# Staging the compressed-key tokens in a ring of four tiles, and nine new durations in the emission estimate of a four-mixer decoder layer

## The chip, the core and the metric

The kernel runs on one core of a Trainium2 chip. The metric is the device time of one execution, in microseconds. The engines are named as the profile names them: PE is TensorE (PEld its weight loads), DVE is VectorE, ACT is ScalarE, POOL is GpSimd, and SP is SyncE, whose queue issues all DMAs here.

## What is computed

One layer over 2048 tokens of width 1024: a normalised input times one combined projection, four groups of four heads, a gate, and an output projection added to the input.

```python
h = rms_norm(x, norm_w) @ w_in          # columns split among the four groups and the gate
o_a = dilated_attention(...)            # A: windows 128/1, 512/4, 2048/16, merged by their softmax sums
o_b = banded_attention(..., 127, sink)  # B: sliding window with sinks
o_c = diff_attention(...)               # C: two causal softmax maps, p0 - lam * p1
# D: three branches of one head group, weighted with sigmoid gates
kc, vc = compress(d_kc, ...), compress(d_vc, ...)        # 127 compressed keys and values
o_cmp = softmax(q @ kc.T + bias) @ vc
idx = top_k(sum over heads of the compressed weights, 16) # 16 of 32 blocks of 64 keys
o_slc = softmax over the selected blocks;  o_win = banded_attention(..., 511)
y = concat(o_a, o_b, o_c, o_d) * silu(gate)
x = x + y @ w_out
```

`compress` adds a position term to the raw keys and values of group D in two versions (one for the first 16 tokens of a block of 32, one for the last 16) and puts them through a small network.

## The kernel before

All engines' instructions are emitted by one program that keeps an estimate of each engine's clock (`T["PE"]`, `T["DVE"]` and so on). `op(engine, ns, after)` advances an estimate, and returns when a result would be there. The time given to `op` costs the chip nothing; it decides only **in which order** the instructions are written into the engines' queues. `defer(ready, f)` puts work off until TensorE's estimate passes `ready`. `drive` runs the attention units of a group and chooses, at each step, among the candidates that the estimate holds for ready: closing a unit, the products with the values, the transposes of the weights, the next scores. Only when none is ready by the estimate does `fill_step` put in a piece of a filler. Fillers are the projection of the groups (`project`: three matmuls for each of eight 128-row pieces of the width, line 833, written C, D, A, B) and the output projection (line 2148). Since every engine works its queue in order, a wrong estimate becomes a wait on the chip.

The stages follow each other so: the projection of C alone, then group C with the projections of C, D and the start of A as fillers, group D (window branch, compressed branch at line 1428, selected branch at line 943 with `Qs`), and groups A and B, with the output projection as filler.

Tiles that are written again and again are rings. `alloc(tag, bufs)` and `release` keep the estimate's record of when a ring's oldest tile comes free. Three rings matter here:

- `sq`, one tile of 128x512. Each projected row tile is squared into it by ACT (line 664) and summed by DVE (line 674).
- `raw`, four tiles of 128x512. The weights of the projections are loaded into them before they are split in a high and a low part (lines 618 and 622), and later the output weights and the gate.
- `pt`, three PSUM banks, for all transposes.

For every fourth row tile of the projection, `turn` transposes four row tiles into a `pt` bank. For the last column block of group D (raw keys and values) the inner function `version(v, e)` adds the position term into an `sq` tile (line 775, DVE), stores it to DRAM (`tc`, through SP), and only when that store has landed by the estimate does the second version take `sq`; then the `pt` bank is given back. This happens four times: blocks p = 0 to 3.

In the compressed branch, `largest` (lines 1471 to 1483, on DVE) chooses the blocks of keys of 128 queries, and `turn_ng` transposes the result (line 1489). `weigh` works out the branch's weights (lines 1277 and 1278), and `o_turn` turns the output back (line 435) and adds its two halves, either on DVE alone (line 439) or on ACT and DVE (lines 442 and 444), whichever the estimate holds to be done first.

## Time and profile before

| | |
|---|---|
| median of three runs | 1796.22 us (1788.68 to 1797.0) |
| the profiled execution, its own time | 1786.75 us |
| span from its first to its last instruction | 1785.0 us |
| busy: PE, DVE, ACT, POOL | 1715.9, 1332.7, 1072.1, 688.4 us |
| mean granted clock of TensorE | 0.986 of full speed |

The profile is of one execution. Between its first and its last instruction lie 1785.0 us, and 1.75 us of its time lie outside. An engine's busy time is the time in which it has an instruction running; what is left of the span is time in which it waits.

### The profile page before, as it was taken

What the parts mean: (1) busy time and instruction counts of PE and PEld (TensorE: products, weight loads), DVE (VectorE), ACT (ScalarE), POOL (GpSimd) and SP (SyncE); (2) the same over time, 40 slices, a digit from 0 to 9 for tenths busy, and PEclk for the clock granted to TensorE, in tenths of its full rate; (3) what the DMA queues carried; (4) which work ended last, traced back from release to release, by engine and by line L of the source; (5) the groups of instructions that cost most, each with busy time, mean ns of one, the idle gap of its engine ahead of it and who ended that gap; (6) DMA issues with size and microseconds to landing.
All of it is one profiled execution on the core that took longest, in us unless ns stands there. A gap on an engine that the chain in (4) does not pass through costs nothing.

```text
span 1785.0 us, 31766 instructions
## 1 busy us (share of the span) xinstructions
PE 1715.9 (96%) x10035; PEld 1503.3 (84%) x10035; DVE 1332.7 (75%) x4072; ACT 1072.1 (60%) x2586; POOL 688.4 (39%) x841
## 2 busy tenths in 40 slices
PE   7989999999998999899989999999999999999999
PEld 5878878888787888688877889999879998888887
DVE  5446778998899996688567778887167777888883
ACT  4445556666676765567555667676256776576661
POOL 4666564544454554112353632222521111423231
PEclk9999999999999999999998999999999999999999
DMA  7763554344446324831485333323375768999986
GB/s 244 227 206 115 165 170 159 99 125 138 125 130 202 100 93 144 229 102 57 142 250 180 123 93 86 109 62 96 103 239 163 233 209 266 293 326 304 303 280 215
DMA packets 283480, 308.24 MB, mean 173 GB/s; under 512 B 80256, under 2 KB 201216, under 8 KB 282640
## 3 DMA queue, kind: packets, MB, share of 16 engines
q1 hardware_dynamic: 283312, 306.21, 55.7%
q8 instruction: 80, 1.31, 0.3%
q14 instruction: 88, 0.72, 0.1%
HBM read 219.47 MB, written 86.92 MB: 172 GB/s over the span
## 4 chain that ended last, share of the span: by engine, by line
PE 44%; DMA 4%; DVE 4%; issue 3%; POOL 2%; SPq 1%; ACT 1%; POOLq 0%; DVEq 0%; ACTq 0%
PE o L422 8%; PE j L833 8%; PE j L2148 7%; PE pt L393 7%; PE s L943 4%; PE s L1639 3%; PE pt L435 2%; PE s L1329 1%; DMA wb<-tkA 1%; SPq L156 1%; DMA DQ<-tqD 1%; PE s L1428 1%; PE pt L2112 1%; POOL xl L577 1%; PE s L1941 0%
## 5 line engine op out<-in xcount | busy, mean ns | idle before, releaser
L833 PE MATMUL j<-wb,xh 128*128 128x512 f32 (+2 forms) x2048 | 619.4, 383 | 12.6 <-ACT wb L618 8.0
L833 PEld LDWEIGHTS j<-wb,xh 128*128 128x128 f32 x2048 | 372.4, 191 | 58.6 <-issue 12.2
L833 PE MATMUL j<-wb,xl 128*128 128x512 f32 (+2 forms) x1024 | 386.1, 377 | 1.3 <-POOL xl L577 1.3
L403 DVE TENSOR_TENSOR pl<-pt,ph 128x512 fp32r<-128x512 f32 (+4 forms) x486 | 312.0, 659 | 40.6 <-ACT ph L399 40.2
L399 ACT ACTIVATE ph<-pt 128x512 fp32r<-128x512 f32 (+4 forms) x486 | 265.3, 575 | 123.5 <-PE pt L393 116.8
L833 PEld LDWEIGHTS j<-wb,xl 128*128 128x128 f32 x1024 | 194.7, 190 | 27.7 <-POOL xl L577 2.7
L679 POOL TENSOR_TENSOR ss<-ss,expo 128x6 f32<-128x6 f32 (+2 forms) x64 | 117.1, 1829 | 213.6 <-DVE ss L677 202.3
L577 POOL TENSOR_TENSOR xl<-xt,xh 128x512 fp32r<-128x512 f32 x112 | 150.1, 1340 | 9.3
L371 ACT ACTIVATE ot<-o 128x512 f32<-128x512 f32 (+1 forms) x160 | 81.5, 509 | 108.9 <-PE o L422 108.4
L943 PE MATMUL s<-keys,Q 128*128 128x512 f32 (+3 forms) x320 | 113.1, 400 | 10.9 <-DVE mx L945 5.5
L2102 POOL TENSOR_TENSOR xt<-xt,sq 128x512 f32<-128x512 f32 x32 | 41.3, 1289 | 197.9 <-DVE sq L2100 85.8
L571 POOL TENSOR_SCALAR xh<-xt 128x512 fp32r<-128x512 f32 x128 | 85.5, 668 | 76.4 <-DMA xt<-in_xt_dram 47.5
L660 ACT ACTIVATE stqk<-j 128x512 f32<-128x512 f32 x64 | 38.3, 598 | 122.5 <-PE j L833 122.3
L945 DVE CUSTOM_DVE_ANT_0 prow<-s,Hs 128x512 f32<-128x512 f32 (+3 forms) x160 | 94.6, 606 | 18.1 <-PE s L943 11.4
L674 DVE TENSOR_REDUCE ss<-sq 128x6 f32<-128x384 f32 (+2 forms) x64 | 39.4, 616 | 92.0 <-ACT sq L664 91.9
L1059 DVE SCALAR_TENSOR_TENSOR pa<-pb,ra,pa 128x1024 f32<-128x1024 f32 (+4 forms) x96 | 103.5, 1105 | 2.3
L945 DVE CUSTOM_DVE_ANT_0 pa<-s,H 128x512 f32<-128x512 f32 (+3 forms) x160 | 93.7, 604 | 14.4 <-PE s L943 12.6
L1655 ACT ACTIVATE ap<-ap,AO 128x128 f32<-128x128 f32 (+1 forms) x192 | 86.4, 454 | 18.6 <-DVE AO L1649 16.7
L945 DVE CUSTOM_DVE_ANT_0 pb<-s,H 128x512 f32<-128x512 f32 (+3 forms) x160 | 92.8, 604 | 4.3 <-PE s L943 3.5
L435 PE MATMUL pt<-ident,ot 128*128 128x128 f32 x512 | 85.4, 279 | 5.2 <-ACT ot L371 5.0
L1043 ACT ACTIVATE pa<-pa,nm 128x128 f32<-128x128 f32 (+7 forms) x64 | 76.9, 1201 | 21.6 <-DVE nm L951 21.1
L1523 ACT ACTIVATE prow<-prow,nm 128x128 f32<-128x128 f32 (+7 forms) x64 | 76.8, 1201 | 15.3 <-DVE nm L951 7.3
(266 smaller groups left out, 4201.7 us busy)
## 6 DMA issues: line engine op xcount, KB each, us to landing
xt<-in_xt_dram SPq DMA_DIRECT2D x128, 256.0 KB, 3.5
xr<-in_x_dram SPq DMA_DIRECT2D x16, 512.0 KB, 5.6
Q<-tqC SPq DMA_DIRECT2D x64, 128.0 KB, 3.4
DQ<-tqD SPq DMA_DIRECT2D x16, 512.0 KB, 4.5
raw<-gate_d SPq DMA_DIRECT2D x32, 256.0 KB, 4.3
stqk<-in_x_dram SPq DMA_DIRECT2D x32, 256.0 KB, 4.8
acc_d<-stqk SPq DMA_DIRECT2D x32, 256.0 KB, 4.5
stqk<-acc_d SPq DMA_DIRECT2D x32, 256.0 KB, 4.1
```

Source lines behind the costliest of these rows:

```text
L393: PE.transpose(ps[:rows, x * 128:(x + 1) * 128], src(), ident)
L399: A.activation(ph[:rows, :n], ps[:rows, :n], AF.Copy)
L403: V.tensor_tensor(pl[:rows, :n], ps[:rows, :n], ph[:rows, :n], op=OP.subtract)
L422: PE.matmul(u["po"][:, c0:c0 + wd], lhsT=lhsT(), rhs=x[:rows, col:col + wd], start=u["k"] == 1, stop=u["k"] == total, skip_group_check=True)
L435: PE.transpose(ps[:, i * 128:(i + 1) * 128], ot[:, i * 128:(i + 1) * 128], ident)
L577: G.tensor_tensor(l, xt, h, op=OP.subtract)
L679: G.tensor_tensor(ss[:, :nh], ss[:, :nh], expo[:, :nh], op=OP.pow)
L833: PE.matmul(ps[:, :n], lhsT=xx[:, ks], rhs=W[k][ww][:, lo:hi], start=(k == 0 and i == 0), stop=(k == KT - 1 and i == 2))
L943: PE.matmul(ps[:, :n], lhsT=q(), rhs=k[:, k0:k0 + n], start=(i == 0), stop=(i == np_ - 1))
L945: V.tensor_tensor_reduce(st["row"][:, k0:k0 + n], ps[:, :n], rev(H, t * 128 + 127 - k0, n), 1.0, LOW, OP.add, OP.max, st["mx"][:, ci:ci + 1])
L1059: V.scalar_tensor_tensor(rows[i][:, k0:k0 + n], part[i][:, k0:k0 + n], ra[:, 1:2], rows[i][:, k0:k0 + n], op0=OP.mult, op1=OP.add)
L2148: PE.matmul(ps, lhsT=xx[:, ks], rhs=OW[half, (k, c)][ww], start=(x == 0 and k == 0 and i == 0), stop=(x == len(halves) - 1 and k == 3 and ...
```

## The change

Two things are changed, and a third follows from the first.

1. Blocks p = 0, 1 and 2 of `version` take a tile of the `raw` ring in place of `sq`. Both versions are then written one directly behind the other, without waiting for the first store, and the `pt` bank is given back behind the second. Block p = 3 stays on `sq`.
2. Nine durations that are given to `op` are replaced: those of the row scales at the start (900 to 1046), of the weights' merge in group C (330 to 447), of `weigh` (400 to 557), of `largest` (3200 to 3412), of the position add (602 to 944), of GpSimd's closing work in C (1850 to 1966) and of the merges in A (5880 to 6826, 450 to 663, 1850 to 2027).
3. The output weights and the gate now keep account of the `raw` ring in the estimate (`alloc`, `release`, and a condition in `prepare`).

```diff
             def version(v, e):
-                hd = alloc("sq", 1)
-                xs = px.tile([128, 512], F32, name="sq", bufs=1)
+                p = t3 // 4
+                if p < 3:
+                    hd = None
+                    xs = px.tile([128, 512], F32, name="raw", bufs=4)
+                else:
+                    hd = alloc("sq", 1)
+                    xs = px.tile([128, 512], F32, name="sq", bufs=1)
                 V.tensor_tensor(xs..., ps..., post..., op=OP.add)
-                e = op("DVE", vv(512), max(e, hd[2]))
+                e = op("DVE", 944.0, max(e, hd[2] if hd else 0.0))
                 if v:
                     give(slot, e)
                 def go():
-                    p = t3 // 4
                     e2 = mv(TC[v][:, :, p * 32:(p + 1) * 32], xs...)
-                    release(hd, e2)
                     stored_one("T", g, p)
-                    if v == 0:
-                        defer(e2, lambda: version(1, e2))
+                    if hd:
+                        release(hd, e2)
+                        if v == 0:
+                            defer(e2, lambda: version(1, e2))
                 defer(e, go)
+                if v == 0 and not hd:
+                    version(1, e)
             version(0, e)
...
-            op("DVE", 400.0)
+            op("DVE", 557.0)
...
-                e = op("DVE", 3200.0, e)
+                e = op("DVE", 3412.0, e)
...
         def load(i, after=0.0):
             k, c = OCH[i]
+            hd = alloc("raw", 4)
             rw = px.tile([128, 512], F32, name="raw", bufs=4)
```

The instructions themselves are the same in number and shape on PE and POOL and in SP's DMAs; on DVE and ACT a few output turns change between lines 439 and 442/444. Nearly everything else is a matter of order. From the start of group C to the end of the projection the order differs in many places; from the last projection matmul of B on it is the same again for a stretch on PE and DVE, and it differs once more in groups A and B. Lines of the changed kernel are up to 11 higher: 840 is the projection (833 before), 780 the position add (775), 952 the scores (943 and 945), 1435 and 1496 the compressed scores and the transpose of the choice (1428 and 1489).

First DVE in the third block. Before, the second position add stands here, 20 rows behind the first, among the scores of group C (`pa`, `pb` are its rows of weights):

```order
L945 ISA pa_1089,mx<-s,H 128x512
L945 ISA mx 128x1
L945 ISA pa_1089,mx<-s,H 128x384
L945 ISA mx 128x1
L775 TENSOR_TENSOR sq<-pt,post 128x32x16
L945 ISA pa_1089,mx<-s,H 128x256
L945 ISA mx 128x1
L951 TENSOR_REDUCE nm<-mx 128x1
```

In the changed kernel both adds stand together, with the score row `pb` ahead and the split `tl` of the key block behind them:

```order
L1066 SCALAR_TENSOR_TENSOR pa_1091<-pb,ra,pa_1091 128x768
L952 ISA pb,mx<-s,H 128x512
L952 ISA mx 128x1
L780 TENSOR_TENSOR raw<-pt,post 128x32x16 x2
L757 SCALAR_TENSOR_TENSOR tl<-pt,gains,th 128x512
L1090 RECIPROCAL rd<-den 128x2
L444 TENSOR_TENSOR O<-O,pt 128x128
L952 ISA pb,mx<-s,H 128x384
L952 ISA mx 128x1
```

The two adds are now one piece of DVE work, and nothing between them waits for a store.

Second PE in the compressed branch. Before, the output turn (435), the transposes of two units' weights (393, `pc`), the transpose of a choice (`ng`) and the next scores stand together, with a few projection matmuls around them:

```order
L833 MATMUL j<-wb,xh 128x416 x2
L833 MATMUL j<-wb,xl 128x416
L435 MATMUL pt<-ident,ot 128x128 x4
L393 MATMUL pt<-ident,pc_11383 32x128 x4
L393 MATMUL pt<-ident,pc_11436 32x128 x4
L1489 MATMUL pt<-ident,ng 32x128
L1428 MATMUL s<-KC,DQ 128x96 x16
L833 MATMUL j<-wb,xh 128x416 x2
L833 MATMUL j<-wb,xl 128x416
L833 MATMUL j<-wb,xh 128x416 x2
L833 MATMUL j<-wb,xl 128x416
L1489 MATMUL pt<-ident,ng 32x128
```

In the changed kernel 11 groups of projection matmuls (33 instructions) and the first `ng` stand between that output turn and the two transposes of `pc`; this is the end of that piece:

```order
L840 MATMUL j<-wb,xl 128x416
L840 MATMUL j<-wb,xh 128x416 x2
L840 MATMUL j<-wb,xl 128x416
L393 MATMUL pt<-ident,pc_11451 32x128 x4
L840 MATMUL j<-wb,xh 128x416 x2
L840 MATMUL j<-wb,xl 128x416
L393 MATMUL pt<-ident,pc_11470 32x128 x4
L1435 MATMUL s<-KC,DQ 128x96 x16
L1496 MATMUL pt<-ident,ng 32x128
L840 MATMUL j<-wb,xh 128x416 x2
```

Counted over the whole branch, from the first to the last row of the compressed scores, 171 projection matmuls stood on PE before and 198 stand there now; 594 were left for the selected branch, and 549 are left now.

Third PE at the end of the compressed branch in the changed kernel, where two units are closed with one group of projection matmuls among them:

```order
L422 MATMUL o<-ph,VC 128x512
L422 MATMUL o<-pl,VC 128x512
L393 MATMUL pt<-ident,pc_12324 128x128 x4
L840 MATMUL j<-wb,xh 128x416 x2
L840 MATMUL j<-wb,xl 128x416
L1435 MATMUL s<-KC,DQ 128x64 x8
L435 MATMUL pt<-ident,ot 128x128 x4
L422 MATMUL o<-ph,VC 128x512
L422 MATMUL o<-pl,VC 128x512
L1435 MATMUL s<-KC,DQ 128x64 x8
L435 MATMUL pt<-ident,ot 128x128 x4
L741 MATMUL pt<-ident,stqk 128x128 x4
```

Before, five groups of projection matmuls stood between the transposes of these weights and the output turn behind the second of these scores; now it is one.

## Rows read from the trace of the kernel before

**Rows 1.** The page: the span, the busy time of TensorE and of VectorE over the span with its share and instructions, and TensorE's granted clock in 40 slices (tenths).

```profile
span 1785.0 us, 31766 instructions
PE 1715.9 (96%) x10035; PEld 1503.3 (84%) x10035; DVE 1332.7 (75%) x4072; ACT 1072.1 (60%) x2586; POOL 688.4 (39%) x841
...
PEclk9999999999999999999998999999999999999999
```

**Rows 2.** The waits of TensorE over the whole span: who waited <- for whom: us in total, times, longest us.

```profile
PE s L943 <- DVE mx L945: 12.0, 10, 3.5
PE j L833 <- ACT wb L618: 8.0, 2, 7.2
...
PE pt L393 <- DVE o L444: 2.9, 1, 2.9
...
PE pt L393 <- DVE sq L775: 0.6, 1, 0.6
```

**Rows 3.** The tiles `sq` and `raw`: operations with count, duration in ns (min/median/max) and first and last start; then, of `sq`, what idle time before its operations ended with (us, times); then, of `raw`, when the projection weights are loaded into it.

```profile
L775 DVE TENSOR_TENSOR sq<-pt,post x8: 1046/1111/1125, 310.5 to 559.0; 128x512 f32<-128x512 f32 x8
...
  DMA tc<-sq: 13.5, 4
...
L156 SPq DMA_DIRECT2D raw<-in_w_D_dram x16: 328/328/1302, 197.1 to 234.5; - x16
L156 SPq DMA_DIRECT2D raw<-in_w_A_dram x16: 327/333/584, 505.4 to 539.6; - x16
```

**Rows 4.** The third block of four row tiles, in order of time, of VectorE, SyncE, ScalarE, TensorE (start us, us, engine line op out<-in, and in brackets the idle time before it and what ended it). `x1` and the like is how many equal instructions the row merges.

```profile
457.82 1.10 DVE L775 TENSOR_TENSOR sq<-pt,post 128x512 f32<-128x512 f32 x1
...
462.71 0.55 SPq L156 DMA_DIRECT2D tc<-sq  x1
...
466.60 0.52 ACT L664 ACTIVATE sq<-stqk 128x384 f32<-128x384 f32 x1 [6.42 <-DMA tc<-sq]
...
468.71 0.39 PE L943 MATMUL s<-keys,Q 128*128 128x256 f32 x1 [3.50 <-DVE mx L945]
...
469.05 1.11 DVE L775 TENSOR_TENSOR sq<-pt,post 128x512 f32<-128x512 f32 x1
```

**Rows 5.** The first block (TensorE) and the second (ScalarE, TensorE), the same columns.

```profile
321.45 0.55 PE L393 MATMUL pt<-ident,pa 128*128 128x128 f32 x3 [0.65 <-DVE sq L775]
...
385.62 0.53 ACT L664 ACTIVATE sq<-stqk 128x384 f32<-128x384 f32 x1 [3.02 <-DMA tc<-sq]
...
387.70 0.39 PE L422 MATMUL o<-pl,VS 128*128 128x256 f32 x1 [0.34 <-DVE pl L403]
```

**Rows 6.** Stretches of the span: from:to, its length, then busy us (and instructions) of PE, PEld, DVE, ACT and POOL, the mean granted clock of TensorE, the DMA engines' share, GB/s.

```profile
465.21:468.71 3.50, 0.00 (x1) 0.00 (x1) 1.44 (x5) 2.11 (x5) 0.58 (x1) 1.00 0.56 110
469.20:472.60 3.40, 3.40 (x17) 3.21 (x15) 3.29 (x7) 2.19 (x7) 2.92 (x4) 0.54 0.32 51
...
936.80:950.50 13.70, 11.00 (x36) 8.45 (x37) 9.54 (x45) 6.23 (x21) 1.34 (x2) 0.51 0.76 234
1026.00:1029.50 3.50, 0.81 (x4) 0.33 (x3) 0.30 (x2) 0.00 (x0) 1.31 (x2) 0.97 0.99 338
1029.50:1033.00 3.50, 3.47 (x11) 2.85 (x12) 2.22 (x10) 1.72 (x6) 0.00 (x0) 0.55 0.54 174
...
1250.00:1300.00 50.00, 50.00 (x252) 44.52 (x251) 9.20 (x24) 12.78 (x25) 26.88 (x30) 1.00 0.39 122
```

**Rows 7.** The compressed branch, in order of time, TensorE and then VectorE.

```profile
933.57 0.65 PE L435 MATMUL pt<-ident,ot 128*128 128x128 f32 x4
...
938.00 1.03 PE L393 MATMUL pt<-ident,pc 128*32 128x128 f32 x4 [2.93 <-DVE o L444]
...
940.74 3.65 PE L1428 MATMUL s<-KC,DQ 128*128 128x96 f32 x16 [1.50 <-DMA DQ<-tqD]
...
933.14 0.86 DVE L1471 SCALAR_TENSOR_TENSOR pn<-pn 128x384 f32<-128x384 f32 x1 [0.20 <-ACT pn L1466]
...
936.95 0.18 DVE L1483 TENSOR_SCALAR ng<-im 128x32 f32<-128x32 f32 x1
...
937.53 0.41 DVE L444 TENSOR_TENSOR o<-o,pt 128x256 f32<-128x256 f32 x1
```

**Rows 8.** The projection on TensorE at the full clock: the start of one group of three matmuls (two with `xh`, one with `xl`) and the start of the next group.

```profile
902.04 0.62 PE L833 MATMUL j<-wb,xh 128*128 128x512 f32 x2
...
902.73 0.62 PE L833 MATMUL j<-wb,xh 128*128 128x512 f32 x2
```

**Rows 9.** The start of the selected branch: SyncE, VectorE, TensorE.

```profile
1025.94 0.47 SPq L156 DMA_DIRECT2D yp_d<-Y  x1
...
1029.17 0.29 DVE L945 CUSTOM_DVE_ANT_0 prow<-s,Hs 128x128 f32<-128x128 f32 x1 [5.65 <-DMA yp_d<-Y]
...
1029.53 0.69 PE L943 MATMUL s<-keys,Qs 128*128 128x384 f32 x1 [2.71 <-DVE mx L945]
```

**Rows 10.** Group A: a multiplication on GpSimd and a subtraction on VectorE beside it, all the executions of that subtraction (count, ns min/median/max), and the TensorE row behind them.

```profile
1530.76 2.42 POOL L1756 TENSOR_TENSOR AO<-AO 128x1040 f32<-128x1040 f32 x1
...
1530.93 2.28 DVE L1864 TENSOR_TENSOR amm<-amn,AO 128x8 f32<-128x8 f32 x1
...
L1864 DVE TENSOR_TENSOR amm<-amn,AO x16: 172/174/2282, 1530.9 to 1733.1; 128x8 f32<-128x8 f32 x16
...
1535.70 0.33 PE L435 MATMUL pt<-ident,ot 128*128 128x128 f32 x1 [2.83 <-ACT ot L371]
```

More of the change, by code (lines that the diff above doesn't have):

```diff
@@ L654, in go @@
                 G.tensor_tensor(rr[:, t:t + 1], ss[:, 0:1], expo[:, 0:1], op=OP.pow)
-                op("POOL", 900.0, e)
+                op("POOL", 1046.0, e)
             return defer(r, go)
@@ L1055, in mix @@
                 V.scalar_tensor_tensor(ra[:, 1:2], den[:, i, 0:1], nlam, ra[:, 0:1], op0=OP.mult, op1=OP.mult)
-                op("DVE", 330.0, e)
+                op("DVE", 447.0, e)
                 for k0 in range(0, nk, 1024):
@@ L1095, in rest @@
                     G.tensor_tensor(O, O, subln.unsqueeze(1).broadcast_to([128, 2, 64]), op=OP.mult)
-                    e3 = op("POOL", 1850.0, e2)
+                    e3 = op("POOL", 1966.0, e2)
                     last.append(defer(e3 + (LATE if (h, t0) != (3, 14) else 0.0), lambda: mv(dv(y_d["C"])[:, t0:t0 + 2, h * 64:h * 64 + 64], O)))
@@ L1757, in one @@
                         G.tensor_copy(O[:, :, 65], mn)
-                        e3 = op("POOL", 3 * 1900.0 + 180.0, e2)
+                        e3 = op("POOL", 6826.0, e2)
                         release(h16, e3)
@@ L1877, in two @@
                 V.tensor_tensor(ms, ms, mn.unsqueeze(1).broadcast_to([128, 2, 4]), op=OP.mult)
-                e2 = op("DVE", 450.0, e1)
+                e2 = op("DVE", 663.0, e1)
                 for i in range(2):
@@ L1883, in two @@
                 G.tensor_tensor(Y[:, :, half], R[:, 0, :, 0:64], R[:, 1, :, 0:64], op=OP.add)
-                e3 = op("POOL", 2 * 580.0 + 690.0, e2)
+                e3 = op("POOL", 2027.0, e2)
                 def go():
@@ L2031, in load, with split @@
             k, c = OCH[i]
+            hd = alloc("raw", 4)
             rw = px.tile([128, 512], F32, name="raw", bufs=4)
             r0 = ROW0[half] + k * 128
-            e = mv(rw, a["w_out"][r0:r0 + 128, c * 512:(c + 1) * 512], after)
+            e = mv(rw, a["w_out"][r0:r0 + 128, c * 512:(c + 1) * 512], max(after, hd[2]))
             if half == "CD" and i in olocked:
-                oparked[i] = (e, lambda: split(i, rw, e))
+                oparked[i] = (e, lambda: split(i, rw, e, hd))
             else:
-                defer(e, lambda: split(i, rw, e))
-        def split(i, rw, e):
+                defer(e, lambda: split(i, rw, e, hd))
+        def split(i, rw, e, hd):
             h, l = places[i]
@@ L2048, in low @@
                 oready[half, OCH[i]] = op("DVE", vv(512) + 62.0, e)
+                release(hd, oready[half, OCH[i]])
                 if i + OAHEAD < 8:
@@ L2071, in prepare @@
             n = at_["load"]
-            while n < min(len(PARTS), at_["part"] + 3) and (n < 2 or n - 2 in zready) and there(*PARTS[n]):
+            while n < min(len(PARTS), at_["part"] + 3) and (n < 2 or n - 2 in zready) and there(*PARTS[n]) and free("raw", 4) < INF:
                 load(n)
@@ L2081, in load @@
                 mv(yt[:, i * 256:(i + 1) * 256], y_d[g][rows, :])
+            hg = alloc("raw", 4)
             gt = px.tile([128, 512], F32, name="raw", bufs=4)
-            e = mv(gt, gate_d[rows, ROW0[half]:ROW0[half] + 512])
-            defer(e, lambda: gate(n, yt, gt, e))
+            e = mv(gt, gate_d[rows, ROW0[half]:ROW0[half] + 512], hg[2])
+            defer(e, lambda: gate(n, yt, gt, e, hg))
         def r_load(n):
@@ L2091, in r_load, with gate @@
                 mv(R[n, c][0], src[t * 128:(t + 1) * 128, c * 512:(c + 1) * 512])
-        def gate(n, yt, gt, e):
+        def gate(n, yt, gt, e, hg):
             hd = alloc("sq", 1)
@@ L2101, in rest @@
                 e2 = op("DVE", vv(512), e)
+                release(hg, e2)
                 G.tensor_tensor(yt, yt, th, op=OP.mult)
```

## Prediction, made before the changed kernel had run

> **What bounds the kernel now.** I read the page first: TensorE is busy 1715.9 us of a span of 1785.0, VectorE 1332.7 [rows 1]. TensorE is the bound, its instructions stay the same in number and shape, so the change can only move two things: the 69.1 us (1785.0 less 1715.9) in which TensorE waits, and the time in which it works at the half clock. The clock row shows one slice at 8 and the rest at 9 tenths or more, so half-clock stretches are short and have to be looked for one by one. Second, the list of TensorE's waits, to see which of them the change can reach: the scores of group C and of the selected branch waiting for row maxima, ten times 12.0 us with a longest of 3.5, the output turn of the compressed branch once 2.9, and one transpose behind the first position add 0.6 [rows 2]. The 8.0 us for the split weights [rows 2] are the kernel's start and the first load, which the change doesn't reach. Third, I follow each reachable wait back in order of time on all engines, and last I take the granted clock behind each wait from windows, since a wait costs twice where the clock falls after it.
>
> **Staging in raw.** In the third block the first add runs at 457.82 (1.10 us), its store is issued at 462.71, and the squaring of the next row tile on ScalarE, which needs the `sq` tile, starts only at 466.60 after 6.42 us of idle time ended by that store; the second add comes at 469.05 [rows 4]. ScalarE works in order, so what stands behind the squaring (exponentials of group C) waits too, and TensorE stands still for 3.50 us at 468.71, for the row maximum behind them [rows 4]. Straight after it the window 469.20 to 472.60 is filled with 3.40 us of work at a granted clock of 0.54 [rows 6], the lower of the two levels, 1.2 GHz; at the full one that work takes 1.70. Before the fall TensorE had stood still from 465.21 to 468.71 [rows 6]. So this block costs 3.50 + 1.70 = 5.2 us. In the changed kernel the squaring no longer shares a tile with the store, and the wait's cause is gone. The first block gives back 0.65 on TensorE; in the second ScalarE waits 3.02 us, but only 0.34 of it arrives at TensorE [rows 5]. I take 0.6 + 0.3 + 5.2 = **6.1 us**. Bounds: nothing, if another wait takes its place in the same stretch, and 11.0, if what ScalarE waited for these stores were all on the path. That is 13.5 us in four waits [rows 3], of which 4.06 are left for the first and the fourth block; the fourth stays on `sq`, and I leave it the larger part, 2.5.
>
> What the move can cost. Two adds are now one piece of 2.2 us (1.10 + 1.11 [rows 4]) on VectorE; queued behind it is a split of keys and then a score row with its maximum. TensorE has the projection to do meanwhile; I charge nothing, and 1.1 us a block, 3.3 in all, if that cover is missing. Only one store more is in flight at a time, on SP's queue, with the same count of DMAs. The `raw` ring could make the adds wait, but the weights of D are loaded until 234.5 and those of A from 505.4 [rows 3], and the three blocks at about 310, 380 and 458 lie between: nothing. If A's first loads waited, it would be for a store that the block at 458 has issued 40 us earlier.
>
> **The compressed branch.** On VectorE `largest` begins at 933.14 and ends at 937.13 (936.95 + 0.18): 4.0 us; only then does the addition of the output turn follow (937.53, 0.41 us) [rows 7]. On TensorE the output turn itself is done at 934.22, and the next transposes, which need its PSUM bank, wait 2.93 us for that addition; after them the scores wait 1.50 us for the load of DQ [rows 7]. The window of 13.7 us around both is at 0.51, 11.00 us busy [rows 6]: again the lower level, after the wait, so 11.00 / 2 = 5.5 us are lost to the clock. In the changed order eleven groups of projection matmuls stand between the output turn and those transposes. At the narrowest spacing of a full group, 0.69 us [rows 8], scaled to 416 columns, that is 11 x 0.69 x 416/512 = 6.2 us of work, more than 2.93 us. So the wait is covered, and without a standstill the clock should stay up, as it does at 1.00 through the 50 us from 1250 [rows 6]: 2.93 + 5.5 = 8.4, of which I take **8**; the load's 1.50 I leave, since no row says when it will be issued. Bounds: nothing, if the wait only moves to the next `largest`, and 9.9 with the load.
>
> The projection is a fixed stock: 27 more of its matmuls (198 less 171) are spent in this branch, and 45 (594 less 549) are missing in the selected one. There the stretch 1250 to 1300 shows TensorE busy all 50 us with VectorE busy 9.20 [rows 6]: this is stock done with nothing to hide. Spending 45 x 0.23 = 10 us of it elsewhere (0.23 is a third of the 0.69 of a group) costs nothing as long as these 50 us last.
>
> **The clock's price.** The Trainium skill, "TensorE: Matmul & The Clock Gate", section "Terms", prices slow time as the whole throttled time times the share of pulses left out. For the 13.7 us that gives 6.8 in place of 5.5, and the sum would be 1.3 us lower. The trace speaks for the busy share, since in 2.70 of those microseconds there was no work to slow.
>
> **The boundary at 1026.** TensorE waits 2.71 us for the first scores with `Qs`, behind the store of the last compressed output (1025.94) [rows 9], and then works 3.47 us at 0.55 [rows 6], which is 1.6 lost: 4.3 in all. The changed order has three other DMAs between that store and the load of `Qs`, where one stood. TensorE had no projection to fill in before and may have none after. I take **1**; bounds 0 and 4.3.
>
> **The rest of the order.** From the start of group C to the end of the projection, and again in A and B, rows stand in another order because the estimate is another. No row shows what new waits this makes. The nearest is a wait such as the third block's: 3.50 alone, 5.2 with its clock. I charge one, rounded, **+3**, for the old order's waits there were the survivors of one particular order and a new order draws new ones; bounds two such waits lost or gained, -10 to +10. The corrected durations themselves say little: `largest` was given as 3200, took about 4000 and is now 3412.
>
> **Sum.** -6.1 - 8 - 1 + 3 = -12.1 us against the profiled execution's own time of 1786.75 (span 1785.0 and 1.75 around it): 1774.6, or -0.68%. The median of the runs shown is 1796.22, 0.5% above the profiled one; the same share of it gives **1784**.
>
> **Rivals.** *Only the staging pays.* The stock moved within the compressed branch is missing where it was taken from, and the 4.0 us chain of `largest` meets another transpose. For it: the dense piece at the end of the branch now has one group of projection matmuls where five stood. Then -6.1 - 1 + 3 = -4.1, or 1792, within 0.5%.
>
> *Collisions of VectorE and GpSimd.* In group A a subtraction of 128x8, whose median is 174 ns, took 2282 once; it ran from 1530.93 to 1533.21 and ended with GpSimd's multiplication (1530.76 + 2.42 = 1533.18), and TensorE lost 2.83 us behind it [rows 10]. The new durations of GpSimd's merges shift 16 such subtractions against them. If three more meet, 3 x 2.83 = 8.5: -12.1 + 8.5 = -3.6, or 1792.6. Against it: one in 16 met so far. That a VectorE operation with two SBUF inputs and a GpSimd operation that reads SBUF hold each other off for a whole instruction is what the Trainium skill states, "SBUF — State Buffer", section "SBUF: two separate sides"; this row agrees, with 2.28 us. It speaks against the change, which writes other pairs of this kind beside each other.
>
> *Slower.* At the end of the compressed branch the changed order closes two units on TensorE with one group of projection matmuls among them. If each of the last four output turns there waits out a whole `largest` (4.0 us), that is 16 us, and the 11.0 us of work among them go at the half clock, +5.5: 21.5. Then -12.1 + 21.5 = +9.4, or 1805.7. It decides from about 21 us on (12.1 given back and 9 more), so it takes all four; two of them would bring no change. For it: the meeting at 938.00 had just this form [rows 7]. Against it: the list of waits has one such wait in the whole branch [rows 2].
>
> *The staging does nothing*, because a `raw` tile is still held: against it are the load times above. Then -8 - 1 + 3 = -6, or 1790.2.
>
> **Chances and range.** Forecast (0.5 to 1.2% faster) 0.52, only staging 0.22, collisions 0.08, slower 0.15, staging without effect 0.03. A change of 0.5% (9 us) is about what a measurement of this kernel can tell: its three runs spread over 0.46%. The second, third and fifth are "same": faster 0.52, same 0.33, slower 0.15. The likeliest case alone is 1776 to 1790: its upper edge is one more wait of 5.2 us (-6.9), its lower edge the staging at 11.0 and the boundary at 4.3 (-20.3). The range takes in the rivals at 1790 to 1793 with the same 5.2 us on top, and below it reaches to the rest of the order at its own lower bound (-10 for +3, together -25.1, or 1771): **1770 to 1798**.
>
> **What will show it.** Right: no store of `tc` ends ScalarE's idle time in the first three blocks, only once for the fourth; the two adds stand 1.1 us apart with no 3.5 us gap of TensorE near 468; between 930 and 950 TensorE runs without a gap over 1.5 us at a clock near 1.00; about 63 us of waits in the span where there were 69.1. Wrong: a gap of over 2 us on TensorE near the adds for a maximum that stands behind both; the 2.9 us of the compressed branch appearing again at another choice, above all in its last 20 us; merges in A over 2 us more than once; loads of A waiting for `raw`; a selected branch in which TensorE has idle time between 1250 and 1300.

## The result, and the profile after

The changed kernel takes 1771.05 us (median of four runs, 1765.34 to 1774.45) against 1795.62 before (four runs, 1788.68 to 1797.0): a ratio of 0.9872, interval 0.985 to 0.9894. By the ratio that is 1.28% or 23.0 us faster; the two medians lie 24.6 us apart. The forecast was 1784, in a range from 1770 to 1798. Its profiled execution takes 1773.27 us, 13.5 less than the profiled one of before; why the medians lie 24.6 apart and these two only 13.5 is the subject of the fifth experiment.

The page after, beside [rows 1]: span, engines, granted clock of TensorE in 40 slices.

```profile
span 1771.5 us, 31769 instructions
PE 1709.5 (97%) x10035; PEld 1503.3 (85%) x10035; DVE 1338.3 (76%) x4072; ACT 1072.3 (61%) x2588; POOL 692.8 (39%) x841
...
PEclk9999999999999999899999999999999999999999
```

TensorE waits 62.0 us (1771.5 less 1709.5), where it waited 69.1. It is busy 6.4 us less for the same instructions. The lower clock explains only a part of that: half of TensorE's busy time under it, an estimate of what it cost, is 20.5 us before and 19.0 after. Where the rest comes from no view shows. The waits after, beside [rows 2] (who <- for whom: us, times, longest):

```profile
PE j L840 <- DVE wb L622: 9.6, 9, 3.1
PE j L840 <- ACT wb L618: 9.0, 3, 8.1
PE s L950 <- DVE mx L952: 8.9, 14, 1.7
...
PE s L950 <- DVE ra L1061: 2.2, 1, 2.2
```

The waits for an output turn's addition (2.9) and behind the first position add (0.6) are gone. The waits of C's and the selected branch's scores for a row maximum are shorter: 8.9 us in all, none over 1.7, where the longest was 3.5 and the total 12.0. What grew is the wait for split weights, 9.6 us in nine pieces against 3.9 before.

The position adds, beside [rows 3] (line, tile, count: ns min/median/max, first and last start):

```profile
L780 DVE TENSOR_TENSOR raw<-pt,post x6: 1025/1102/1124, 313.7 to 462.9; 128x512 f32<-128x512 f32 x6
L780 DVE TENSOR_TENSOR sq<-pt,post x2: 1021/1077/1133, 547.2 to 554.2; 128x512 f32<-128x512 f32 x2
```

In order of time on VectorE and TensorE, the first and the third block (start, us, engine, line; in brackets the idle time and what ended it), beside [rows 4, 5]:

```profile
313.66 1.89 DVE L780 TENSOR_TENSOR raw<-pt,post 128x512 f32<-128x512 f32 x2
315.40 0.15 DVE L1061 RECIPROCAL ra<-den 128x1 f32<-128x1 f32 x1
...
315.72 0.77 PE L950 MATMUL s<-keys,Q 128*128 128x384 f32 x2 [2.25 <-DVE ra L1061]
...
462.00 2.04 DVE L780 TENSOR_TENSOR raw<-pt,post 128x512 f32<-128x512 f32 x2
```

The compressed branch, TensorE and then VectorE, beside [rows 7]:

```profile
938.26 0.66 PE L435 MATMUL pt<-ident,ot 128*128 128x128 f32 x4
...
946.15 0.60 PE L393 MATMUL pt<-ident,pc 128*32 128x128 f32 x4
...
947.51 1.97 PE L1435 MATMUL s<-KC,DQ 128*128 128x96 f32 x16
...
941.65 0.18 DVE L1490 TENSOR_SCALAR ng<-im 128x32 f32<-128x32 f32 x1
...
942.23 0.41 DVE L444 TENSOR_TENSOR o<-o,pt 128x256 f32<-128x256 f32 x1
```

The start of the selected branch, SyncE, VectorE, TensorE, beside [rows 9]:

```profile
1029.36 0.32 SPq L156 DMA_DIRECT2D yp_d<-Y  x1
...
1034.54 0.29 DVE L952 CUSTOM_DVE_ANT_0 prow<-s,Hs 128x128 f32<-128x128 f32 x1 [1.42 <-PE s L950]
...
1033.89 0.35 PE L840 MATMUL j<-wb,xl 128*128 128x416 f32 x1
1034.08 0.22 PE L950 MATMUL s<-keys,Qs 128*128 128x128 f32 x1
```

And three stretches, beside [rows 6] (length, then busy us and instructions of PE, PEld, DVE, ACT, POOL, granted clock, DMA share, GB/s):

```profile
460.00:475.00 15.00, 15.00 (x88) 13.46 (x87) 14.55 (x40) 10.69 (x29) 11.06 (x17) 1.00 0.56 140
935.00:955.00 20.00, 19.99 (x122) 17.25 (x122) 15.68 (x77) 13.31 (x53) 8.60 (x10) 1.00 0.93 292
1025.00:1037.00 12.00, 12.00 (x64) 10.62 (x63) 4.75 (x16) 3.15 (x9) 9.88 (x12) 1.00 0.39 128
```

The reader is to see this. Around the third block TensorE is busy all 15 us at 1.00, where it stood still for 3.50. In the compressed branch the choice now ends at 941.83 and the addition of the output turn at 942.64, which is 3.7 us behind the end of the output turn itself (938.92); but TensorE comes to the next transposes only at 946.15, behind its eleven groups of projection, and the clock stays at 1.00. At the boundary the last output store is issued at 1029.36; TensorE works on projection until 1034.08, and by then nothing has to be waited for. In the first block TensorE waits 2.25 us, and the view names a reciprocal that stands behind both adds. But the second load of `Q`, which these scores read, was issued at 310.80 and landed at 315.58, within 0.01 us of that reciprocal, so the view can't tell the two apart. Another profile can. The eighth experiment has the same order in group C, and there TensorE and VectorE show this:

```profile
313.05 0.59 PE L950 MATMUL s<-keys,Q 128*128 128x384 f32 x2 [1.90 <-DMA Q<-tqC]
...
313.12 0.17 DVE L1061 RECIPROCAL ra<-den 128x1 f32<-128x1 f32 x1
```

The scores start before the reciprocal does, so they don't need it; nor do they need the adds, which end at 313.29 there. What TensorE waited for is the load.

**By stages.** The same borders can be read in every profile: the first score of C (line 943, tile `Q`), the first of the window branch (1329), the first of the compressed branch (1428), the end of the last projection matmul (833). Runs that share an order within a stage give several profiles of it, so the table has means over them, with their number and spread. (The experiments below are among them.)

| stage | old order, us | new order, us |
|---|---|---|
| group C | 603.7 (4 profiles, 601.9 to 606.1) | 602.9 (4, 599.7 to 604.8), with 24 projection matmuls more done |
| window branch | 199.1 (4, 197.8 to 200.6) | 199.2 (6, 198.0 to 201.1), with 6 fewer |
| compressed and selected branch to the last projection | 397.4 (7, 396.9 to 398.3) | 378.1 (5, 377.8 to 378.5), with 18 fewer |
| rest of A and B | 475.3 (8, 472.5 to 478.6) | 472.0 (6, 470.7 to 473.2) |

A projection matmul costs 0.19 to 0.23 us [rows 8]. At equal work the change is therefore worth about -5.6 us in C (603.7 less 602.9, and 24 x 0.2), +1.3 in the window branch, -15.7 in the compressed and selected branch, and -3.3 in A and B: -23.3, close to the -23.0 of the ratio and the -24.6 of the medians. The start ahead of group C is not in the table; it took 114.9 to 117.8 us in all 14 profiles.

### The profile page after: what moved, and what is told of

Same layout as the page of the kernel before. It is cut to its first block, busy times and chain, and to the rows that moved or that the text cites. A ratio compares the mean times of both kernels' runs of the same rounds, so it can differ in the third digit from the quotient of the medians.

```text
span 1771.5 us, 31769 instructions
## 1 busy us (share of the span) xinstructions
PE 1709.5 (97%) x10035; PEld 1503.3 (85%) x10035; DVE 1338.3 (76%) x4072; ACT 1072.3 (61%) x2588; POOL 692.8 (39%) x841
## 4 chain that ended last, share of the span: by engine, by line
PE 51%; DVE 3%; issue 1%; DMA 1%; ACT 1%; POOL 0%; SPq 0%; DVEq 0%; POOLq 0%
PE j L840 11%; PE j L2159 9%; PE o L422 9%; PE pt L393 8%; PE s L1646 4%; PE s L950 4%; PE pt L435 3%; PE s L1336 1%; PE pt L2123 1%; PE s L1948 1%; PE s L1435 1%; PE pt L741 0%; DVE pl L403 0%; PE j L1164 0%; DMA xt<-in_xt_dram 0%
## 5 line engine op out<-in xcount | busy, mean ns | idle before, releaser
L840 PEld LDWEIGHTS j<-wb,xh 128*128 128x128 f32 x2048 | 373.1, 190 | 67.4 <-DVE wb L622 14.5
L1066 DVE SCALAR_TENSOR_TENSOR pa<-pb,ra,pa 128x1024 f32<-128x1024 f32 (+4 forms) x96 | 107.5, 1147 | 2.3
L1050 ACT ACTIVATE pb<-pb,nm 128x128 f32<-128x128 f32 (+7 forms) x64 | 76.8, 1200 | 16.5 <-DVE nm L958 16.3
```

The source lines that it names most:

```text
L840: PE.matmul(ps[:, :n], lhsT=xx[:, ks], rhs=W[k][ww][:, lo:hi], start=(k == 0 and i == 0), stop=(k == KT - 1 and i == 2))
L1050: A.activation(row[:, :nk], row[:, :nk], AF.Exp, bias=nm, accum_out=den[:, i, m:m + 1])
```

## The experiments

All edits are to the emission program. Where an experiment's order agrees word for word with another kernel's in some stage, this is said, since then a difference there is not one of order.

**The tile alone.** The kernel before, with `raw` for `sq` in blocks 0 to 2 and the estimate left as it was.

```diff
                 hd = alloc("sq", 1)
-                xs = px.tile([128, 512], F32, name="sq", bufs=1)
+                xs = px.tile([128, 512], F32, name="raw", bufs=4) if t3 // 4 < 3 else px.tile([128, 512], F32, name="sq", bufs=1)
```

> The kernel before, with only the physical tile of blocks 0 to 2 exchanged (raw for sq); the estimate is told the old thing, so every instruction stands where it stood. The prediction's theory (the shared tile is what costs 3.5 us of standstill and 1.7 us of slow clock in the third block): the gap at 468.7 goes, and the time falls by 4 to 6 us, to a ratio of 0.9967 +- 0.001. The rival (the wait would be taken over by the next one on the same engines, since the second add still stands 20 rows later and the bank is held as long): less than 2 us, ratio 0.999 to 1.001.

Measured: ratio 0.9953 (0.9937 to 0.9968), 1786.15 us against 1795.11. ScalarE's waits for the store fall from 13.5 us in four [rows 3] to one:

```profile
ACT sq L664 <- DMA tc<-sq: 2.5, 1, 2.5
```

In the stretch of the third block the wait of 3.50 us and the low clock are gone; 1.9 us of waits remain in it, 1.32 of them for another addition of VectorE (line 444). A wait 40 us ahead of it, 0.48 us in the first profile of before and 1.59 in the second, is 2.4 now, for a load of keys:

```profile
PE s L943 <- DMA keys<-tkC: 2.4, 1, 2.4
```

```profile
460.00:475.00 15.00, 13.09 (x84) 11.50 (x83) 14.70 (x41) 9.90 (x24) 8.83 (x14) 1.00 0.68 160
```

The tile theory holds: with the tile exchanged and every instruction in its old place, most of what the third block lost comes back. The stage of group C took 597.9 us, 5.8 less than the mean of the old order, beside 6.1 forecast for it; by the medians of the whole kernel it was even 9.0.

**Staging taken back.** The changed kernel with blocks 0 to 2 on `sq` again; its order differs only within C.

```diff
-                p = t3 // 4
-                if p < 3:
-                    hd = None
-                    xs = px.tile([128, 512], F32, name="raw", bufs=4)
-                else:
-                    hd = alloc("sq", 1)
-                    xs = px.tile([128, 512], F32, name="sq", bufs=1)
+                hd = alloc("sq", 1)
+                xs = px.tile([128, 512], F32, name="sq", bufs=1)
...
-                if v == 0 and not hd:
-                    version(1, e)
```

> The changed kernel with blocks 0 to 2 back on sq; all new durations and the accounting of raw stay. Its order differs from that of the changed kernel only within group C. The prediction's theory: slower than the changed kernel by about 6 us, all of it in the stage of group C, ratio to the kernel before 0.990 to 0.991. The rival, taken from the two traces (the stage of group C did not become shorter): as fast as the changed kernel within 3 us, ratio 0.986 to 0.989, with new waits of the changed order as large as those taken away.

Measured: 0.9887 (0.9869 to 0.9904), 1774.21 us, so 0.15% or 2.7 us slower than the changed kernel; the intervals overlap. That is the rival's figure. In this order ScalarE never waits for a store of `tc`: the new durations alone have moved the adds. But TensorE has two long waits that the changed kernel doesn't have (near the first the changed kernel has six short ones instead, none over 1.3 us and 5.5 together; near the second none):

```profile
PE j L833 <- DVE wb L622: 3.6, 1, 3.6
...
PE pt L393 <- DVE pa L1059: 3.0, 1, 3.0
```

**The two durations of the compressed branch taken back.** The changed kernel with them at their old values; in C, A and B its order is that of the changed kernel.

```diff
-            op("DVE", 557.0)
+            op("DVE", 400.0)
...
-                e = op("DVE", 3412.0, e)
+                e = op("DVE", 3200.0, e)
```

> The changed kernel with only two durations set back: that of the compressed branch's weights (557 to 400) and that of the choice of blocks (3412 to 3200). The order then differs from that of the changed kernel only in the three branches of group D, where it is close to the kernel before again. The prediction's theory: slower than the changed kernel by 9 us (8 in the compressed branch and 1 at the boundary), ratio to the kernel before 0.992 to 0.993. The rival from the traces: slower by 15 us, because the compressed branch and the start of the selected one gave back 15.0 us of waits and slow clock, ratio 0.995 to 0.997.

Measured: 0.9953 (0.9935 to 0.9972): of 1.28% faster, 0.47% are left, and 0.81% or 14.5 of the 23.0 us are gone. That is the rival's 15 rather than the prediction's 9. Its waits in the compressed and the selected branch are those of before again:

```profile
PE pt L393 <- DVE o L444: 2.9, 1, 2.9
PE s L950 <- DVE mx L952: 2.9, 1, 2.9
PE s L1435 <- DMA vvA<-vst: 2.4, 1, 2.4
```

The stage took 397.4 us, as before.

**The staging alone.** The kernel before with `version` as in the changed kernel (the add's 944 included).

> The kernel before with the staging part alone (blocks 0 to 2 in raw, both adds together, the add's duration 944); all other durations old. The order differs from the kernel before only within group C and the last projection of D. The prediction's theory: -6 us and up to one new wait of 5, ratio 0.996 to 0.9995. The rival: no gain in group C, ratio 0.999 to 1.002.

Measured: 0.9981 (0.9967 to 0.9996), 1791.16 against 1795.11, so 4.0 us: within the first theory's span, and less than the 9.0 that the tile alone gave in the first run. The interval also touches the rival's span.

**The kernel before, profiled again.**

> The kernel before, profiled once more, because its profiled execution (1786.75 us) was shorter than all of its timed runs since (1789 to 1800). If the profile of before is typical, the time is spread evenly and no stage differs by over 2 us; if it was a lucky one, one or two stages (the window branch above all, where four other profiles show 10 to 14 us at the half clock and this one 6.8) are 3 to 8 us longer, by the clock and not by waits.

Measured: 1797.87 us, 11.1 more than the first profile. The instructions and their order are the same, so the two pages can be laid side by side with [rows 1]:

```profile
span 1796.1 us, 31766 instructions
PE 1723.8 (96%) x10035; PEld 1513.8 (84%) x10035; DVE 1332.1 (74%) x4072; ACT 1071.3 (60%) x2586; POOL 687.8 (38%) x841
...
PEclk9999999999999999899998999999999999999999
```

TensorE is busy 7.9 us longer and waits 3.2 us longer. The busy part goes with the clock: half of the busy time under the lower clock is 34.7 us here and 20.5 in the first profile. (These differ by 14.2, more than the 7.9, so half is too high a price.) In groups A and B this execution has a stretch under the lower clock in which TensorE was busy nearly all the time, and another around the wait of 2.83 us behind an output turn of A (the last row):

```profile
1415.00:1425.00 10.00, 9.79 (x49) 9.55 (x49) 7.21 (x27) 7.34 (x25) 4.59 (x4) 0.66 0.49 153
...
1400.00:1470.00 70.00, 68.99 (x428) 67.28 (x428) 52.70 (x206) 51.17 (x176) 14.06 (x9) 0.93 0.74 231
...
1530.00:1560.00 30.00, 27.17 (x150) 23.53 (x149) 23.40 (x61) 12.49 (x36) 15.17 (x16) 0.89 0.96 295
```

Where the same work stands in the first profile, the clock was full:

```profile
1385.00:1460.00 75.00, 73.99 (x482) 71.43 (x481) 59.34 (x234) 57.95 (x200) 14.08 (x9) 1.00 0.74 236
...
1520.00:1550.00 30.00, 27.17 (x166) 23.25 (x164) 26.23 (x74) 14.94 (x46) 15.17 (x16) 1.00 0.93 287
```

So the expectation that one or two stages of D would hold it was only partly right: A and B held most (478.6 us against 472.5), C 3.0, the window branch 1.6. In C it was waits, and not the clock alone: the wait of the first block for the position add, 0.65 us in [rows 5], is 2.85 here, and that of the third block 2.23 where it was 3.50. The order is the same in both, so the difference is one between executions; on the first profile the change looks smaller (13.5) than on the medians (24.6). The forecast was made against that profile and carried over to the median by its share.

**The two durations alone.** The kernel before with only 557 and 3412.

> The kernel before with only the two durations of the compressed branch changed (weights 400 to 557, choice 3200 to 3412): the other half of the run with these two set back. Group C, A and B keep their order; that of group D is another again (137 fewer matmuls of the projection before the selected branch than the changed kernel has). Theory that the better durations themselves put cover where the chip needs it: 10 to 15 us faster, ratio 0.992 to 0.9945. Rival, that the changed kernel's order in D is one lucky draw: less than 5 us either way, ratio 0.997 to 1.003.

Measured: 0.9963 (0.9949 to 0.9977), 6.6 us faster: between the two expectations. Group D's order is a third one here, and its waits are others:

```profile
PE pt L393 <- DVE rdc L1463: 3.4, 1, 3.4
PE o L422 <- DVE pl L403: 2.8, 1, 2.8
PE pt L741 <- DVE tl L757: 2.4, 1, 2.4
```

The boundary's wait is gone; 8.6 us of others have come, one of them again on transposes of weights (393). So what the two durations are worth depends on the order that they are put into: 6.6 us here, 14.5 in the changed kernel.

**No choice.** The kernel before, old order, with the choice of blocks left out except for its last operation (the selected branch then works with a wrong choice).

```diff
-                V.scalar_tensor_tensor(pn..., FMIN, pn..., op0=OP.is_ge, op1=OP.mult)
-                ...
-                V.tensor_scalar(ng, im, -1.5e30, NEG, op0=OP.is_gt, op1=OP.mult)
+                V.tensor_scalar(ng, selc, -1.5e30, NEG, op0=OP.is_gt, op1=OP.mult)
```

> The kernel before in its old order, with the choice of blocks left out on VectorE (the eight pieces of 2.9 to 4.0 us; only the last operation stays, on the constant instead of the sums), so that the selected branch works with a wrong choice. Nothing else moves. The prediction's price of 8.4 us for that one meeting in the compressed branch (2.93 of wait and 5.5 of slow clock): 8 us faster, ratio 0.995 to 0.996, no gap of 2.9 us near 935 and no half clock from 937 to 951. Rival, that the load of DQ behind it (1.50 us) alone keeps the clock down: 2 to 4 us, ratio 0.998 to 0.999, with the half clock still there.

Measured: 1.0 (0.9985 to 1.0015). Neither theory. The choice is gone from in front of the addition, and yet TensorE waits 2.23 us of its 2.93 (VectorE, ScalarE, TensorE):

```profile
934.50 0.17 DVE L1472 TENSOR_SCALAR ng<-selc 128x32 f32<-128x32 f32 x1
...
935.55 0.32 DVE L1278 TENSOR_TENSOR wt<-wt,sg 128x4 f32<-128x4 f32 x1
938.47 0.42 DVE L444 TENSOR_TENSOR o<-o,pt 128x256 f32<-128x256 f32 x1 [2.60 <-ACT o L442]
...
938.07 0.36 ACT L442 ACTIVATE o<-pt 128x256 f32<-128x256 f32 x1
...
938.94 0.61 PE L393 MATMUL pt<-ident,pc 128*32 128x128 f32 x4 [2.23 <-DVE o L444]
```

VectorE is ready at 935.87 and stands idle for 2.60 us. What it waits for is ScalarE's half of the same output turn, behind eight exponentials. In the kernel before that half was late as well:

```profile
936.43 0.36 ACT L442 ACTIVATE o<-pt 128x256 f32<-128x256 f32 x1
```

It ended at 936.79, only 0.34 us before the choice (937.13 [rows 7]). Two engines were late at once; the trace names the later one. Taking it away shortened the wait by 0.70 us, and the kernel's time did not move. The clock stays low:

```profile
935.00:960.00 25.00, 20.96 (x82) 15.63 (x82) 10.61 (x41) 12.46 (x48) 5.75 (x9) 0.66 0.63 197
```

**A and B taken back.** The changed kernel with the three merges of A at their old durations and without the accounting of `raw`; its order differs only in A, B and the output projection.

> The changed kernel with the three merges of A at their old durations and without the accounting of the raw ring; its order differs from that of the changed kernel only in groups A and B and the output projection. The prediction charged all such redrawing with +3 us and had a rival in which three more merges of A collide with GpSimd. Theory that A and B contribute next to nothing: within 3 us of the changed kernel, ratio 0.986 to 0.989. Rival, that the new merges are a part of the gain (the wait of 2.83 us at 1533 is gone in the changed kernel's trace): 3 to 6 us slower than the changed kernel, ratio 0.989 to 0.991.

Measured: 0.9878 (0.9854 to 0.9902), 1771.79 us: as fast as the changed kernel. (The profile of this run has 475.3 us in A and B against 472.0 in the mean of the new order, but its median does not show it.)

**The four durations of C alone.** The kernel before with 1046, 447, 944 and 1966; its order in C is that of the run without staging.

> The kernel before with only the four durations of group C changed (row scales, merge of the weights, position add, closing work); blocks 0 to 2 stay on sq, group D, A and B keep their old order and durations. Its order in group C is that of the run without staging. If the position add's 944 alone already moves the third block's wait out of the way (the run without staging shows no wait for its store): 3 to 6 us faster, ratio 0.9965 to 0.998. Rival, that these durations do nothing and the staging carries what group C gave: ratio 0.999 to 1.001.

Measured: 1.002 (1.0007 to 1.0033), 3.4 us slower, on the far side of the rival: these durations by themselves give nothing and cost a little.

**The tile in the new order.** The run without staging, word for word in order, with the tile of the first run.

> The run without staging, word for word the same order, with only the tile of blocks 0 to 2 exchanged (raw for sq): the same edit as in the first run, on the new durations. Theory that the tile is worth what it hid: in this order no wait of ScalarE for the store is left, so it is worth nothing, within 2 us of the run without staging, ratio 0.988 to 0.990. Rival, that the tile is worth 6 us or more wherever it is put: ratio 0.985 to 0.986.

Measured: 0.9907 (0.9885 to 0.993), 1773.88 us, where the run without staging had 1774.21. By the ratios (0.9907 against 0.9887) it is even 0.2% slower, just outside the theory's span; the intervals overlap. The same edit that gave 9 us in the old order gives nothing in this one, where ScalarE did not wait for the store. At the place of the first block it has a wait as long as the changed kernel's, without two adds standing together, and here too the trace names the load of `Q`:

```profile
PE s L943 <- DMA Q<-tqC: 2.2, 1, 2.2
```

**The second add later.** The changed kernel with `defer(e, lambda: version(1, e))` in place of the direct call.

> The changed kernel, but the second position add is put off until the estimate has the first one done, so that other work of VectorE can stand between them; still no wait for the store. In the changed kernel's profile TensorE waits 2.25 us at 313.5 for a reciprocal that stands behind both adds (1.89 us), and then works 3.4 us at the half clock. Theory that the double piece costs about 3.9 us there: 3 to 4 us faster than the changed kernel, ratio 0.984 to 0.986. Rival, that the new order makes another wait like it: within 2 us, ratio 0.986 to 0.989.

Measured: 0.9892 (0.9873 to 0.9911), no faster than the changed kernel. TensorE still waits 1.90 us at 312.7, for `Q`. The load is late there whether the adds stand together or not, and taking the double piece apart gains nothing. The expectation took the reciprocal for the cause, which it is not.

**The choice at 4000.** The changed kernel with 4000 for 3412.

> The changed kernel with the choice of blocks given as 4000 in place of 3412, about what it took in the profile of before. The order differs only in group D, where 27 matmuls of the projection fewer stand in the compressed branch. If the nearer the duration the better the cover: as fast or 1 to 3 us faster, ratio 0.985 to 0.988. Rival, that the order of the changed kernel in D is one draw among good and bad ones: 4 to 10 us slower, ratio 0.990 to 0.993.

Measured: 0.9908 (0.9893 to 0.9922), 1776.01 us: slower than the changed kernel by about 0.36%, the rival's figure. The compressed and selected branch took 388.2 us to the last projection, 10 more. But this is no test of a duration nearer to the recorded one. The eight choices in the trace of before take 2.89 to 3.98 us from their first to their last operation, 3.32 on average: 3412 is near the average, and 4000 is about the longest of them. A product waited 1.6 us for its weights, and this is the stretch around it, with the lower clock that the changed kernel doesn't have there:

```profile
955.00:985.00 30.00, 27.38 (x131) 22.45 (x130) 18.21 (x84) 18.35 (x71) 12.60 (x17) 0.77 0.45 137
```

None of the twelve was faster than the changed kernel.

## Why the prediction was right, and where its terms were off

**The number** was right by little. 1771 lies 1 us inside the range, below the 1776 to 1790 of the likeliest case, and 1.28% is more than the 0.5 to 1.2% of the forecast. The range reached so low only because of a bound of -10 for the rest of the order. That rest turned out between 0 and -3, and more than half of what the sum lacked lay in the compressed branch and the boundary, as told below. So it is luck that the range held.

**What bounds the kernel** was read right: the instructions of TensorE stayed the same, and it lost less time. Waits of about 63 us were forecast and 62.0 were found, but their places were others. In group C TensorE waits 24.5 us in both pages, where some 4 were to go; the boundary and groups A and B gave more instead.

**Staging, -6.1.** Right in mechanism and near in size for the order of before: with the tile alone the third block's 3.50 us and its slow clock went, the fourth block kept its 2.5 us on ScalarE as supposed (in the changed kernel that wait is gone too), and C's stage lost 5.8. But this is the value of the tile in that order. In the new one the staging was worth 2.7 us when taken back, within the uncertainty, and the tile itself nothing. The stages split C's -5.6 a little further. The run without staging, the one with C's durations alone and the tenth have one order in C, with the same 24 matmuls more, and their stage took 606.3, 606.5 and 607.2 us: about -1.8 at equal work against the old order, and -3.8 more for the changed kernel's 602.9. So in the new order it is the place of the adds and what follows from it that counts, and not the tile; seven profiles, four of them with a spread of 5 us, don't settle the size. (Over the whole kernel the durations alone cost 3.4, the staging alone gave 4.0, and together with A and B they gave some 8.) No charge for two adds together was right: the 2.25 us at the first block, which look like its price, were a load's.

**The compressed branch, -8.** The cover works as worked out: eleven groups lie over a late addition, the transposes come at 946.15, and the clock stays up. (They took 7.5 us, not 6.2, since eight of them have 512 columns and not 416.) Between the first and the last compressed score the waits fell from 5.34 to 2.44 us, and the 7.3 us that the lower clock had cost there by the estimate (half of TensorE's busy time under it) are gone: 10.2. The 1.50 for the load of DQ, which I left in, went too. Wrong was which engine had to be covered: the prediction named the choice on VectorE alone, but ScalarE was 0.34 us from being the cause. Work put over the place hides both; leaving the choice out took 0.70 of the 2.93 us and nothing from the kernel's time.

**The boundary, -1.** This is the term that was mis-sized. The wait of 2.71 and the 1.6 of slow clock both vanished, 4.3 us, the lower bound. The step that failed is "TensorE had no projection to fill in before and may have none after". The order had the answer: between the last compressed score and the first one with `Qs` 81 projection matmuls stood before, and 111 stand there now. The three DMAs in between cost nothing, as the store had 4.7 us to land.

**The rest, +3.** Wrong in sign. A and B gave -3.3 in the profiles (the run that took them back shows 0.7 in its median, so this part isn't settled), the window branch +1.3, and C is told above. A new order was expected to bring one new wait; it brought several small ones and lost others. The sentence on `largest`, "was given as 3200, took about 4000", read one piece of eight: the average is 3.32 us.

**The rivals.** That only the staging pays fell clearly: the branches of D hold 14.5 of the 23.0 us. The dense end of the compressed branch made no wait over 0.7 us. Collisions in A came twice in 16, where there had been one of 2.28 us and a short one of 0.54, beside [rows 10]; first VectorE's two long subtractions, then what GpSimd had running:

```profile
1518.03 1.86 DVE L1871 TENSOR_TENSOR amm<-amn,AO 128x8 f32<-128x8 f32 x1
...
1528.54 1.21 DVE L1871 TENSOR_TENSOR amm<-amn,AO 128x8 f32<-128x8 f32 x1
...
1515.63 4.24 POOL L1761 TENSOR_TENSOR AO<-AO,mg 128x1040 f32<-128x1040 f32 x2 [20.70 <-DMA xt<-yC]
...
1528.44 1.28 POOL L2113 TENSOR_TENSOR xt<-xt,sq 128x512 f32<-128x512 f32 x1
```

The first ends at 1519.89 and GpSimd's second multiplication at 1519.87, the second at 1529.75 and GpSimd's at 1529.72. So the rule of the Trainium skill, "SBUF — State Buffer", section "SBUF: two separate sides", that was weighed as a rival (such a pair excludes each other for a whole instruction) agrees with both, at 1.7 and 1.0 us above the usual 0.17. The time that it would have given did not come: ScalarE waited 2.5 us in all behind them, and the stage is not longer.

**The level.** 12.1 us were forecast from one profile, and the profiles differ by 13.5, but that agreement is chance: by the medians the change is worth 24.6, by the ratio 23.0, and by the means over profiles 23.3. The sum was about half of it. The terms that were too small are the boundary (3.3 short), the compressed branch (2 to 4), and the rest of the order (+3 for what turned out between 0 and -3). The profile that it was set against was 8 us shorter than the median of its kernel (1794.55 over 22 executions); that 1786.75 lay under all three timed runs was to be seen, and the text only scaled it.

## What to carry to other kernels

In a kernel whose order is drawn by an estimate, read the new order at every place where the old trace waits, and count the covering work that now stands there: here two counts (33 matmuls over the output turn, 30 more at the boundary) stand at the waits that held most of the gain. A better number is no gain as such: 944 is nearer than 602 to the position add's recorded 1.1 us, and yet the four durations of C alone made the kernel 3.4 us slower. And before pricing the removal of a wait, look for the next engine or load that is late at the same spot. A view names only the last of them: taking the choice away left 2.23 of 2.93 us to ScalarE, and the wait put down to a reciprocal was a load's.

## What the runs showed of the chip

The clock's part differs between executions of one kernel. Behind the same wait of 2.83 us in group A the clock stayed full in the first profile of before and fell in the second, and at 1415 to 1425 of the second it was granted at 0.66 with TensorE busy 9.79 of 10 us. A price for slow clock that is read from one profile is therefore one draw: over the 14 profiles of all kernels here the lower clock cost between 15 and 35 us, by the estimate of half of TensorE's busy time under it. The estimate is on the high side: the same sixteen scores of the compressed branch took 3.65 us under the lower clock [rows 7] and 1.97 at the full one, 1.85 times and not twice as long.
